# Memory columns between columns of z, weights in pieces of four blocks, six split pairs and a queue model with GpSimd's hold

## The chip, the core and the metric

The kernel runs on one core of a Trainium2 chip. The metric is the device time of one execution in microseconds (us). Engines: PE is TensorE (PEld its weight loads), DVE is VectorE, ACT is ScalarE, POOL is GpSimd, SP is SyncE, on whose queue all transfers are issued here. A block is 128 rows or columns.

## What is computed

One layer of a decoder, for a prompt of 512 tokens and a sample of 8 tokens, which lie side by side as 520 columns. Float32 throughout.

```python
h = rms_norm(x, norm_g);  z = h @ w_in          # 2048 -> 56 blocks of 128 columns
u, gate_pool, qkv (3 groups x q,k,v x 4 heads), gate_dil, q_mem (4 heads), gate_mem = split(z)
mem_kv = rms_norm(mem_prompt, mem_norm_g) @ w_mem_kv        # 256 memory tokens, 8 blocks
y_pool = pool_mix(u)                                        # trailing means 2, 4, 8, 16
y_dil  = 3 groups of banded attention (window, dilation) = (128,1), (512,4), (2048,16), QK-norm, merged per head
y_mem  = attention of q_mem on the memory tokens, QK-norm
y = x + concat(silu(gate_pool)*y_pool, silu(gate_dil)*y_dil, silu(gate_mem)*y_mem) @ w_out   # 12 blocks -> 16 blocks
```

The sample does the same with its own caches, which are copied to the outputs shifted by one row. Outputs are y, the new keys and values, the memory's keys and values and the shifted caches.

## The kernel before

**Layout.** Channels are on the partitions, tokens in the free dimension. A job makes one block of 128 columns of z (or of the memory's keys and values, or of the output): it goes through the 16 blocks of the inner dimension (12 for the output). Each float32 product is done as three products in fp32r: weights and activations are split in a high and a low part, and high times high, high times low and low times high are added. A job of z has 2 sections of 260 columns, so 16 x 3 x 2 = 96 matmuls; a job of the memory has one section of 256 columns and 48 matmuls; a job of the output has 72. There are 56 jobs of z, 8 of the memory and 16 of the output.

**The weights' way.** `emit_raw` loads raw weights into a ring `wraw`. `emit_split` takes four blocks (512 columns) of them: ACT writes the high part `whi`, DVE the low part `wlo` (raw less high). I call this a split; there are 304. One split serves 24 matmuls of a job of z (a piece), or 12 of the memory. The pairs `whi`, `wlo` lie in a ring of `SPB` = 5. `run_jobs` emits one split after each piece, so a split stands in the program three pieces ahead of its use. `wraw` has `RAWB` = 6 tiles of eight blocks (512 KB). When a tile's second half has been split, the next load is issued on SP, and with it, at a rate, copies of the caches (`d2d_q`, up to 712 KB each).

**What sets the order.** The program is in manual order: each engine runs its instructions in the order in which the Python code emits them. Side work (norms, attention, the sample) is written as generators in `tasks`. After each block `tick` advances those whose last step is done by the clock `ck`, a model of the five queues: `use` adds a duration to an engine's queue, and `busy` holds tasks back when ACT or DVE has over 2.5 us of queue beyond PE. `p_ar` is GpSimd's sum or maximum over the partitions, in place, 96 of them; the model books it on `pool` alone.

**Stages.** `run_first` does four jobs of z at once, while the squares of x are summed; then come four jobs (q and k of head 0), during which `mem_prep` scales and splits the memory; then the 8 jobs of the memory, back to back; then 8 gates, and for each head its v, q and k, with `mem_attn`, `dil_attn` and the sample's units (`sample_scores`, `sample_values`; 16 for the memory, 16 for the heads) between them; then the pool's jobs; then the output. The output's first two jobs run together, block by block, since the blocks of y come ready late. An evacuation of a finished job (`q_evac`, `mem_evac`, ...) waits in `pend`, in order of jobs. A dot product of the sample is `sk` (product on DVE), `p_ar(sk)`, `smx` (maximum, DVE), exponentials (ACT), then eleven small DVE instructions (`sz`, `ss`, `sy`, `sv`).

Of the kernel before, what the change touches and what calls it, by code (L numbers as in the profile page):

```python
# [26 lines left out]
NH = 4  # L27
# [21 lines left out]
class Clock:  # L49


    LAT = 0.12

    def __init__(self):
        self.pe = 0.0
        self.free = {"act": 0.0, "dve": 0.0, "pool": 0.0, "sp": 0.0, "hbm": 0.0}
        self.last = 0.0
        self.written = {}
        self.used = {}

# [18 lines left out]
    def use(self, eng, dur, ins, outs):  # L79
# [13 lines left out]
        end = max(self.free[eng], self.after(ins, outs)) + dur  # L93
        self.free[eng] = end
        self.done(end + self.LAT, ins, outs)

# [18 lines left out]
def trunk(ctx, tc, nc, I, O):  # L115
# [66 lines left out]
    def d_red(out, in_, op, axis):  # L182
        nc.vector.tensor_reduce(out=out, in_=in_, op=op, axis=axis)  # L183
        ck.use("dve", nfree(in_) * 0.00104 + 0.08, [in_], [out])
# [7 lines left out]
    def d_recip(out, in_):  # L192
        nc.vector.reciprocal(out=out, in_=in_)
        ck.use("dve", nfree(out) * 0.0083 + 0.08, [in_], [out])
# [59 lines left out]
    free = {"tmp": 3, "sq": 2, "vt": 2, "psb": 4}  # L254
# [76 lines left out]
    def job(src, nkb, lhs, sections, done, wide=True):  # L331
        jobs.append((src, nkb, lhs, sections, done, wide))

    raws = []
    quarters = []
# [4 lines left out]
    RAWB = 6  # L340
    SPREAD = 8
    SPB = 5
# [4 lines left out]
    def build_stream():  # L347

        def pair(j0):
            for k in range(0, jobs[j0][1], 4):  # L350
                for j in (j0, j0 + 1):
                    raws.append((jobs[j][0][:, k:k + 4, :], 4))
                    quarters.append(((j, k), 0, len(raws) - 1))

        for k0, k1 in [(0, 1), (1, 2)] + [(k, k + 2) for k in range(2, KB, 2)]:
            raws.append((I["w_first"][:, FIRST * k0:FIRST * k1, :], FIRST * (k1 - k0)))
            for k in range(k0, k1):
                quarters.append((("first", k), FIRST * (k - k0), len(raws) - 1))
        for j in range(FIRST, len(jobs)):
            nkb = jobs[j][1]  # L360
            if j == first_o:
                pair(j)
            if j in (first_o, first_o + 1):
                continue
            for k0 in range(0, nkb, 8):
                n = min(8, nkb - k0)
                raws.append((jobs[j][0][:, k0:k0 + n, :], n))
                for q in range(k0, k0 + n, 4):
                    quarters.append(((j, q), q - k0, len(raws) - 1))

    def emit_raw():
# [3 lines left out]
        src, n = raws[i]  # L375
# [11 lines left out]
    def emit_split():  # L387
        i = nxt_q[0]
        if i >= len(quarters):
            return  # L390
        nxt_q[0] += 1
        key, off, ri = quarters[i]
        r = raw_t[ri][:, off:off + 4, :]
# [4 lines left out]
        split_t[key] = (hi, lo)  # L398
        if i + 1 >= len(quarters) or quarters[i + 1][2] != ri:
            del raw_t[ri]  # L400
            emit_raw()
# [7 lines left out]
    def run_jobs(group, each=None, before=None):  # L409
        accs = {}  # L410
        for j in group:
            _, _, _, sections, _, wide = jobs[j]
            if wide:
                t = psum_m()
                accs[j] = [t[:, s, 0:c1 - c0] for s, (c0, c1) in enumerate(sections)]
            else:
# [4 lines left out]
        nkb = jobs[group[0]][1]  # L421
        cur = {}
        for k in range(nkb):
            if before:
                before(k)
            for j in group:
                _, _, lhs, sections, _, _ = jobs[j]
                if k % 4 == 0:
                    cur[j] = split_t.pop((j, k))
                whi, wlo = cur[j]  # L430
                mh, ml = lhs(k)
                for a, b, w, m in ((0, 0, whi, mh), (0, 1, whi, ml), (1, 0, wlo, mh)):
                    for s, (c0, c1) in enumerate(sections):
                        mm(accs[j][s], w[:, k % 4, :], m[:, c0:c1],
                           start=(k == 0 and a == 0 and b == 0), stop=(k == nkb - 1 and a == 1))
            if each:
                each(k)
            if k % 4 == 3:
                for _ in group:
                    emit_split()  # L440
            if flags.get("x"):
                while pend and (flags.get("mem") or pend[0][0]):
                    pend.pop(0)[1]()
            tick()
        for j in group:
            pend.append((len(jobs[j][3]) == 2, lambda j=j: jobs[j][4](accs[j])))
# [71 lines left out]
    def mem_evac(i):  # L518
# [12 lines left out]
        def value(acc):  # L531
            need("vt")
            z = row("vt", 2)[:, 0:ML]
# [90 lines left out]
    def v_evac(g, h):  # L624
        def f(acc):
            need("vt")
            z = row("vt", 2)
# [290 lines left out]
    def pool_task(c, u):  # L918
# [5 lines left out]
        while sh < w:  # L924
            nt_ = row("vt", 2)
# [70 lines left out]
    def zjob(cb, done, wide=True):  # L996
        job(I["w_in"][cb], KB, xs, SEC, done, wide)

    for h in range(NH):
        zjob(CB_QM + h, q_first(h), h < 2)  # L1000

    def qk_jobs(h, groups):
        for g in groups:
            zjob(CB_QKV + g * 12 + h, q_evac(g, h))
            zjob(CB_QKV + g * 12 + 4 + h, k_evac(g, h))

    qk_jobs(0, (0, 1))
    first_m = len(jobs)
    for i in range(NM):
        job(I["w_mem"][i], KB, lambda k: (memt[k // 2][0][:, k % 2, :], memt[k // 2][1][:, k % 2, :]),  # L1010
            ((0, ML),), mem_evac(i), False)
    first_q = len(jobs)
    for h in range(NH):
        zjob(CB_GM + h, gate_evac(8 + h, 4 if h == 3 else 0))
    for h in range(NH):
        zjob(CB_GD + h, gate_evac(4 + h, 4 if h == 3 else 0))
    for h in range(NH):
        for g in range(NG):
            zjob(CB_QKV + g * 12 + 8 + h, v_evac(g, h))
        qk_jobs(h, range(NG) if h else (2,))  # L1020
    for c in range(4):
        zjob(CB_GP + c, gate_evac(c, 4 if c == 3 else 0))
    for c in (3, 2, 1, 0):
        zjob(CB_U + c, u_evac(c))
    first_o = len(jobs)
    for m in range(NO):
        job(I["w_out"][m], KO, xs, SEC, o_evac(m), m != 1)
# [13 lines left out]
    RATE = len(d2d_q) / (2.0 * (first_o - first_q) + 1.5 * SPREAD)  # L1041


    with tc.manual_schedule():
# [11 lines left out]
        load_x(1)  # L1056
        emit_raw()
        load_x(2)
        emit_raw()
        load_x(3)  # L1060
        load_x(4)
        emit_raw()
        load_x(5)
        load_x(6)
        emit_raw()
        load_x(7)
# [123 lines left out]
        run_first(each_first)  # L1190
        while not flags.get("x"):
            push()
        j = FIRST
        while j < len(jobs):
            if j == FIRST:
                spawn(mem_prep())
                mem_task = tasks[-1]
            if j == FIRST + 1:
# [5 lines left out]
            if j == first_m:  # L1204
# [3 lines left out]
            if j == first_q:  # L1208
# [3 lines left out]
            if j == first_o - 1:  # L1212
                run_jobs([j], lambda k: split_ready(k))
            elif j == first_o:
# [112 lines left out]
```

## Time and profile before

| | us |
|---|---|
| time before, median of 3 runs | 927.62 (927.02 to 927.92) |
| the profiled execution, its own time | 927.79 |
| its span in the trace | 926.0 |
| PE busy | 894.7 (97%) |
| DVE busy | 672.9 (73%) |
| ACT busy | 388.2 (42%) |
| POOL busy | 285.0 (31%) |
| the 16 DMA engines, mean share | 68.4% |

The span lies 1.8 us under the execution's own time. Ends of matmuls are modelled and overlap, so PE's 97% is not the share of the time in which it could not have been faster; the distance from one start to the next is what a matmul takes. A duration on DVE includes the time for which the instruction was held up after its start.

### The profile page before, as it was taken

How to read it: one execution, taken by the hardware profiler on the slowest of the kernel's cores; microseconds unless marked ns; L12 is line 12 of the kernel's file. 1: busy time of each engine (PE TensorE's matmuls, PEld its weight loads, DVE VectorE, ACT ScalarE, POOL GpSimd, SP SyncE). 2: the span in 40 equal slices, each digit the busy share in tenths (PEclk: the TensorE clock that was granted, in tenths of full speed). 3: DMA queues.
4: the chain of work that ended last, by engine and by line, in shares of the span. 5: the costliest groups of instructions: out<-in, count | busy, mean ns of one | idle time of the engine just before them, and what ended most of it. 6: DMA issues, size and time to landing. Idle time of an engine off the chain costs nothing.

```text
span 926.0 us, 17968 instructions
## 1 busy us (share of the span) xinstructions
PE 894.7 (97%) x7208; PEld 879.2 (95%) x7208; DVE 672.9 (73%) x1225; ACT 388.2 (42%) x795; POOL 285.0 (31%) x96
## 2 busy tenths in 40 slices
PE   7999898999999999999999999989999999999998
PEld 7999888999999999999998999989999899999998
DVE  7678999757888769977698866997659698333231
ACT  7547655443364434444343353245432624222220
POOL 1032544325444424622255322552215220000000
PEclk9999999999999999999999999999999999999999
DMA  9435346897877866578866788668975545899531
GB/s 347 157 114 196 115 154 224 270 341 233 275 222 258 289 223 212 195 260 311 289 233 217 271 300 311 218 221 285 332 253 195 211 137 197 329 389 352 196 104 47
DMA packets 64211, 219.52 MB, mean 237 GB/s; under 512 B 8440, under 2 KB 22648, under 8 KB 61944
## 3 DMA queue, kind: packets, MB, share of 16 engines
q1 hardware_dynamic: 64128, 218.39, 68.4%
q8 instruction: 56, 0.92, 0.4%
q14 instruction: 27, 0.22, 0.1%
HBM read 200.32 MB, written 106.25 MB: 331 GB/s over the span
## 4 chain that ended last, share of the span: by engine, by line
PE 70%; DVE 22%; ACT 3%; issue 3%; DMA 2%; POOL 0%; SPq 0%; DVEq 0%; ACTq 0%
PE psm L205 62%; PE psb L205 8%; DVE wlo L164 7%; DVE sv L187 3%; DVE mx L164 2%; DVE S L164 2%; DVE smx L183 1%; DVE sk L164 1%; ACT whi L154 1%; ACT sk L154 1%; DVE tmp L168 1%; DMA o_kv<-vt 1%; DVE vt L164 1%; DVE qk L164 1%; DVE smx L168 1%
## 5 line engine op out<-in xcount | busy, mean ns | idle before, releaser
L205 PE MATMUL psm<-xh,whi 128*128 128x260 f32 x2088 | 434.0, 288 | 9.2 <-ACT whi L154 8.4
L205 PE MATMUL psm<-xh,wlo 128*128 128x260 f32 x2088 | 426.2, 285 | 9.7 <-DVE wlo L164 9.7
L205 PE MATMUL psm<-xl,whi 128*128 128x260 f32 x2088 | 423.9, 284 | 0.0
L205 PEld LDWEIGHTS psm<-xh,whi 128*128 128x128 f32 x2088 | 326.2, 190 | 16.1 <-ACT whi L154 8.6
L164 DVE TENSOR_TENSOR wlo<-wraw,whi 128x512 fp32r<-128x512 f32 x304 | 270.4, 906 | 96.5 <-ACT whi L154 96.1
L205 PEld LDWEIGHTS psm<-xh,wlo 128*128 128x128 f32 x2088 | 324.8, 190 | 12.1 <-DVE wlo L164 12.0
L205 PEld LDWEIGHTS psm<-xl,whi 128*128 128x128 f32 x2088 | 324.4, 190 | 0.0
L154 ACT ACTIVATE whi<-wraw 128x512 fp32r<-128x512 f32 x304 | 181.0, 621 | 169.0 <-PE psm L205 149.3
L197 POOL PARTITION_ALL_REDUCE sk<-sk x32 | 130.3, 4071 | 130.3 <-DVE sk L164 56.1
L197 POOL PARTITION_ALL_REDUCE sq<-sq x32 | 101.0, 3164 | 186.2 <-ACT sq L154 186.2
L154 ACT ACTIVATE sk<-sk,smx 128x256 f32<-128x256 f32 (+1 forms) x64 | 35.5, 555 | 115.3 <-DVE smx L168 64.8
L197 POOL PARTITION_ALL_REDUCE mx<-mx x17 | 46.4, 2729 | 69.7 <-DVE mx L164 69.3
L164 DVE TENSOR_TENSOR tmp<-psm,vn 128x260 f32<-128x260 f32 x30 | 11.5, 424 | 76.8 <-PE psm L205 58.5
L154 ACT ACTIVATE tmp<-tmp 128x520 f32<-128x520 f32 (+2 forms) x76 | 46.3, 610 | 23.8 <-DVE sq L168 16.5
L154 ACT ACTIVATE sq<-qk 128x520 f32<-128x520 f32 x28 | 17.7, 636 | 85.9 <-DVE qk L164 77.9
L205 PE MATMUL psb<-y,wlo 128*128 128x256 f32 x128 | 37.7, 295 | 6.9 <-DVE wlo L164 6.9
L205 PE MATMUL psb<-y,whi 128*128 128x256 f32 x192 | 42.6, 290 | 0.8 <-ACT whi L154 0.8
L154 ACT ACTIVATE tmp<-sq,eps 128x520 f32<-128x520 f32 (+1 forms) x32 | 22.3, 696 | 33.2 <-POOL sq L197 33.2
L205 PEld LDWEIGHTS psb<-y,whi 128*128 128x128 f32 x192 | 32.9, 196 | 1.0 <-ACT whi L154 1.0
L187 DVE CUSTOM_DVE_ANT_1 sv<-sv,sk,sy 128x384 f32<-128x384 f32 x32 | 33.1, 1071 | 0.6
L205 PEld LDWEIGHTS psb<-y,wlo 128*128 128x128 f32 x128 | 24.9, 194 | 8.9 <-DVE wlo L164 8.8
L168 DVE SCALAR_TENSOR_TENSOR tmp<-sq,tmp 128x520 f32<-128x520 f32 (+1 forms) x32 | 21.6, 675 | 11.6 <-ACT tmp L154 11.6
(129 smaller groups left out, 740.8 us busy)
## 6 DMA issues: line engine op xcount, KB each, us to landing
o_cache<-cache SPq DMA_DIRECT2D x88, 712.0 KB, 7.9
wraw<-w_in SPq DMA_DIRECT2D x104, 512.0 KB, 5.3
o_cache<-cache SPq DMA_DIRECT2D x24, 584.0 KB, 6.6
vn<-xT SPq DMA_DIRECT2D x32, 260.0 KB, 5.7
wraw<-w_mem SPq DMA_DIRECT2D x16, 512.0 KB, 4.0
wraw<-w_out SPq DMA_DIRECT2D x14, 512.0 KB, 6.5
o_zero<-zero SPq DMA_DIRECT2D x6, 1024.0 KB, 8.8
sk<-dks SPq DMA_DIRECT2D x16, 384.0 KB, 3.0
```

Source lines behind the costliest of these rows:

```text
L154: nc.scalar.activation(out=out, in_=in_, func=func, scale=scale, bias=bias, **kw)
L164: nc.vector.tensor_tensor(out=out, in0=in0, in1=in1, op=op)
L168: nc.vector.scalar_tensor_tensor(out=out, in0=in0, scalar=scalar, in1=in1, op0=op0, op1=op1)
L183: nc.vector.tensor_reduce(out=out, in_=in_, op=op, axis=axis)
L187: nc.vector.tensor_tensor_reduce(out=out, in0=in0, in1=in1, scale=1.0, scalar=init, op0=op0, op1=op1, accum_out=accum)
L197: nc.gpsimd.partition_all_reduce(t, t, P, op)
L205: nc.tensor.matmul(out, lhsT=lhsT, rhs=rhs, start=start, stop=stop)
```

## The change

Five things are changed together.

1. **Order of jobs.** Jobs are grouped by hand as lists of pieces (`groups`). The memory's 8 jobs no longer run back to back: each of four jobs of z (v of group 0 and 1, k of group 1, v of group 2, all head 0) is cut in its four pieces, and between these stand the pieces of two memory jobs. So three jobs of z precede the memory instead of four, and three jobs of v move from after it to between it. `mem_prep` is put first among the tasks and starts one group after the first.
2. **Pieces of weights.** `wraw` holds four blocks (256 KB) instead of eight, in 10 tiles instead of 6; each split frees its tile and issues the next load. Loads of weights go from 163 to 304 and all DMA issues from 472 to 613. The copies' rate is set anew.
3. **Six pairs** (`SPB` 5 to 6), and three tiles `vt` instead of two.
4. **The model.** `p_ar` calls `hold`: for the inner part of its duration the model's DVE does not start an instruction, except for those that read PSUM and for reductions and reciprocals. A matmul of 260 columns is 0.120 us in the model instead of 0.111, `p_ar` 10% shorter.
5. **Evacuations.** `pend` lets an evacuation of z pass one of the memory that still waits for the memory's norm. The output's first two jobs alternate by pieces of four blocks instead of by blocks.

```diff
-        ck.use("pool", nfree(t) * 0.00625 + 0.35, [t], [t])
+        ck.use("pool", nfree(t) * 0.00563 + 0.35, [t], [t])
+        e = ck.free["pool"]
+        ck.hold(e - nfree(t) * 0.00563 - 0.1, e - 1.15)
...
+    def hold(self, s, e):
+
+        if s < self.free["dve"]:
+            self.free["dve"] += e - s
+        self.held = [h for h in self.held if h[1] > self.pe] + [(s, e)]
...
-        d = 2 * max(0.107, n / 1200.0) if lhsT.dtype == F32 else max(0.107, (n + 6) / 2400.0)
+        d = 2 * max(0.107, n / 1200.0) if lhsT.dtype == F32 else max(0.107, n * 0.000456 + 0.0015)
...
-    RAWB = 6
+    RAWB = 10
     SPREAD = 8
-    SPB = 5
+    SPB = 6
...
-        t = st([P, 8, P], "wraw", RAWB)
-        load(t[:, 0:n, :], src)
-        raw_t[i] = t
-        d2d["acc"] += d2d["rate"] * n / 8.0
+        raw_t[i] = st([P, 4, P], "wraw", RAWB)
+        load(raw_t[i], raws[i][1])
+        d2d["acc"] += d2d["rate"]
...
-                while pend and (flags.get("mem") or pend[0][0]):
-                    pend.pop(0)[1]()
+                    for p in [p for p in pend if p[0] or flags.get("mem")]:
+                        pend.remove(p)
+                        p[1]()
...
+    for i, (f, a) in enumerate(((v_job, (0, 0)), (v_job, (1, 0)), (k_job, (1, 0)), (v_job, (2, 0)))):
+        j = f(*a)
+        m0, m1 = mem_job(2 * i), mem_job(2 * i + 1)
+        groups.append([(j, 0), (m0, 0), (m0, 4), (j, 4), (m0, 8), (m0, 12),
+                       (j, 8), (m1, 0), (m1, 4), (j, 12), (m1, 8), (m1, 12)])
...
-    RATE = len(d2d_q) / (2.0 * (first_o - first_q) + 1.5 * SPREAD)
+    RATE = len(d2d_q) / (4.0 * (last_g - first_q) + 3.0 * SPREAD)
...
-                spawn(mem_prep())
-                mem_task = tasks[-1]
+                mem_task = [ck.pe, mem_prep()]
+                tasks.insert(0, mem_task)
```

**SP's queue in the memory's stage.** A row is a transfer, out<-in and shape; `w_mem` are the memory's weights, `w_in` those of z. Before:

```order
L215 DMA wraw_1031<-w_mem 128x1024
L215 DMA wraw_1096<-w_mem 128x1024
L215 DMA vn_1154<-memT 128x512
L215 DMA wraw_1172<-w_mem 128x1024
L215 DMA vn_1238<-memT 128x512
L215 DMA wraw_1250<-w_mem 128x1024
```

The same queue in the changed kernel:

```order
L230 DMA sv_973<-mvs 128x512
L230 DMA wraw_1007<-w_mem 128x512
L230 DMA wraw_1054<-w_in 128x512
L230 DMA wraw_1092<-w_mem 128x512
L230 DMA wraw_1131<-w_mem 128x512
L230 DMA wraw_1165<-w_in 128x512
```

The tiles are half as large, a piece of z stands before each two of the memory, and the memory's own columns (`memT`) have moved ahead of this place.

**DVE's queue at head 2.** Here `sk` is the product whose partition sum POOL takes next, `sz` to `y` are one unit of the sample, `wlo` is a split. Before, from the product to the next split:

```order
L164 TENSOR_TENSOR sk_7439<-sk_7439,qs_82 128x768
L164 TENSOR_TENSOR sz_7516<-sz_7516,szs_7517 128x2
L193 RECIPROCAL sz_7516<-sz_7516 128x2
L164 TENSOR_TENSOR ss_7056<-ss_7056,cs_84 128x3x2
L183 TENSOR_REDUCE sy_1080_7519<-ss_7056 128x2
L187 ISA sv_7287,sy_7518<-sv_7287,sk_7285,sy_1080_7519 128x3x128
L187 ISA sy_7518 128x1
L187 ISA sv_7287,sy_7518<-sv_7287,sk_7285,sy_1080_7519 128x3x128
L187 ISA sy_7518 128x1
L164 TENSOR_TENSOR sy_7518<-sy_7518,sz_7516 128x2
L164 TENSOR_TENSOR y_513_3144<-y_513_3144,sy_7518 128x2
L164 TENSOR_TENSOR wlo_7598<-wraw_7052,whi_7597 128x512
```

The changed kernel, around the corresponding product:

```order
L177 TENSOR_TENSOR wlo_7812<-wraw_7405,whi_7811 128x512
L196 TENSOR_REDUCE smx_7830<-sk_7570 128x2
L181 SCALAR_TENSOR_TENSOR smx_7830<-smx_7830,nself_7242 128x2
L177 TENSOR_TENSOR wlo_7856<-wraw_7442,whi_7855 128x512
L177 TENSOR_TENSOR sk_7732<-sk_7732,qs_82 128x768
L177 TENSOR_TENSOR wlo_7888<-wraw_7473,whi_7887 128x512
L177 TENSOR_TENSOR qk_7901<-psm_7749,rsx_72 128x260 x2
L177 TENSOR_TENSOR wlo_7935<-wraw_7513,whi_7934 128x512
```

Before, the unit's small instructions and the evacuation of a job stood between the product and the split, so that the split came last of all; now splits stand directly behind the maximum and behind the product, and the unit has moved to another gap.

**PE's queue at the output's first two jobs.** `psm` and `psb` are the sums of the two jobs, `xh` and `xl` the split blocks of y. Before:

```order
L205 MATMUL psm_9517<-xh_24_87,whi_9441 128x260 x2
L205 MATMUL psm_9517<-xl_40_103,whi_9441 128x260 x2
L205 MATMUL psm_9517<-xh_24_87,wlo_9442 128x260 x2
L205 MATMUL psb_9518<-xh_24_87,whi_9479 128x260
L205 MATMUL psb_9519<-xh_24_87,whi_9479 128x260
L205 MATMUL psb_9518<-xl_40_103,whi_9479 128x260
```

The changed kernel:

```order
L220 MATMUL psm_9780<-xh_24_87,whi_9692 128x260 x2
L220 MATMUL psm_9780<-xl_40_103,whi_9692 128x260 x2
L220 MATMUL psm_9780<-xh_24_87,wlo_9693 128x260 x2
L220 MATMUL psm_9780<-xh_25_88,whi_9692 128x260 x2
L220 MATMUL psm_9780<-xl_41_104,whi_9692 128x260 x2
L220 MATMUL psm_9780<-xh_25_88,wlo_9693 128x260 x2
```

Before, the second job used block 0 of y before block 1 was touched; now the first job goes through blocks 0 to 3 before the second begins.

## Rows read from the trace of the kernel before

**Rows 1.** Chain of work that ended last, merged: start us, us, what.

```profile
6.24 2.98 PE psm L205 x12
...
54.33 46.13 PE psm L205 x384
100.46 2.84 PE psb L205 x24
...
158.48 1.43 PE psm L205 x12
...
454.15 0.89 PE psb L205 x8
...
458.81 0.86 PE psb L205 x4
...
918.41 4.57 PE psm L205 x36
```

**Rows 2.** Timeline of PE, first score matmuls of heads 0 to 3.

```profile
337.97 1.05 PE L205 MATMUL psb<-qk,qk 128*128 128x128 f32 x8
...
453.99 1.05 PE L205 MATMUL psb<-qk,qk 128*128 128x128 f32 x8
...
571.96 1.05 PE L205 MATMUL psb<-qk,qk 128*128 128x128 f32 x8
...
689.17 1.05 PE L205 MATMUL psb<-qk,qk 128*128 128x128 f32 x8
```

**Rows 3.** Stretches: us, busy PE, PEld, DVE, ACT, POOL, PEclk, DMA share, GB/s.

```profile
54.00:100.00 46.00, 46.00 (x385) 46.00 (x385) 42.55 (x68) 29.53 (x57) 13.44 (x4) 1.00 0.51 167
100.00:158.00 58.00, 50.23 (x390) 48.10 (x390) 55.22 (x87) 33.64 (x69) 30.29 (x11) 0.97 0.49 162
...
478.00:532.00 54.00, 50.41 (x398) 49.35 (x397) 47.52 (x85) 22.58 (x52) 22.74 (x6) 0.97 0.74 254
```

**Rows 4.** Waits: engine, line, waited for: us in total, times, longest.

```profile
ACT whi L154 <- PE psm L205: 149.3, 70, 4.4
...
ACT sk L154 <- DVE smx L168: 64.8, 12, 10.1
...
PE psm L205 <- DVE wlo L164: 9.7, 9, 2.6
```

**Rows 5.** Timeline at head 2, rows of POOL, DVE and PE.

```profile
617.05 4.67 POOL L197 PARTITION_ALL_REDUCE sk<-sk  x1 [8.73 <-DVE sz L164]
...
617.36 3.49 DVE L187 CUSTOM_DVE_ANT_1 sv<-sv,sk,sy 128x384 f32<-128x384 f32 x1
...
620.78 0.61 DVE L187 CUSTOM_DVE_ANT_1 sv<-sv,sk,sy 128x384 f32<-128x384 f32 x1
...
624.58 0.80 PE L205 MATMUL psm<-xh,wlo 128*128 128x260 f32 x2 [2.59 <-DVE wlo L164]
```

**Rows 6.** One row of DVE's timeline, a split's low part without a hold.

```profile
612.88 0.68 DVE L164 TENSOR_TENSOR wlo<-wraw,whi 128x512 fp32r<-128x512 f32 x1
```

**Rows 7.** Timeline at head 3, one row of ACT and one of PE.

```profile
731.54 0.62 ACT L154 ACTIVATE sk<-sk,smx 128x384 f32<-128x384 f32 x1 [7.52 <-DVE smx L168]
...
738.93 0.51 PE L205 MATMUL psm<-xh,whi 128*128 128x260 f32 x2 [2.18 <-ACT whi L154]
```

**Rows 8.** DMA: two issues (count, KB, us to landing), two stretches as in rows 3.

```profile
wraw<-w_out SPq DMA_DIRECT2D x14, 512.0 KB, 6.5
...
wraw<-w_out SPq DMA_DIRECT2D x20, 256.0 KB, 6.9
...
6.00:12.00 6.00, 5.76 (x33) 5.76 (x34) 5.62 (x10) 5.68 (x11) 0.52 (x4) 1.00 1.03 396
...
816.00:830.00 14.00, 14.00 (x118) 14.00 (x118) 4.62 (x9) 2.89 (x5) 0.00 (x0) 1.00 1.03 421
```

**Rows 9.** Timeline at the last block of y, two rows of DVE.

```profile
789.30 0.93 DVE L168 SCALAR_TENSOR_TENSOR y<-psb,gains,y 128x260 f32<-128x260 f32 x2 [0.80 <-PE psb L205]
...
790.94 0.70 DVE L164 TENSOR_TENSOR xl<-y,xh 128x520 fp32r<-128x520 f32 x1 [0.70 <-ACT xh L154]
```

More of the change, by code (lines that the diff above doesn't have):

```diff
@@ L59, in __init__ @@
         self.used = {}
+        self.held = []
     def after(self, ins, outs):
@@ L92, in use @@
             return
-        end = max(self.free[eng], self.after(ins, outs)) + dur
+        start = max(self.free[eng], self.after(ins, outs))
+        if eng == "dve" and shared and not any(a.tensor.name.startswith("ps") for a in ins):
+            for s, e in self.held:
+                if s <= start < e:
+                    start = e
+        end = start + dur
         self.free[eng] = end
         self.done(end + self.LAT, ins, outs)
+    def hold(self, s, e):
+        if s < self.free["dve"]:
+            self.free["dve"] += e - s
+        self.held = [h for h in self.held if h[1] > self.pe] + [(s, e)]
     def dma(self, nbytes, ins, outs):
@@ L347, in build_stream @@
     def build_stream():
[L349 to L369, printed above, removed]
+        for k in range(KB):
+            raws.append((("first", k), I["w_first"][:, FIRST * k:FIRST * k + FIRST, :]))
+        for seq in groups[1:]:
+            for j, k in seq:
+                raws.append(((j, k), jobs[j][0][:, k:k + 4, :]))
     def emit_raw():
@@ L407, in flush_pend, with run_jobs @@
             pend.pop(0)[1]()
[L409 to L413, printed above, removed]
+    accs = {}
+    def run_jobs(seq, each=None, before=None):
+        fin = [] if before else pend
+        for j, q in seq:
+            _, nkb, lhs, sections, done, wide = jobs[j]
+            if q == 0 and wide:
                 t = psum_m()
                 accs[j] = [t[:, s, 0:c1 - c0] for s, (c0, c1) in enumerate(sections)]
-            else:
+            elif q == 0:
                 need("psb", len(sections))
@@ L1012, in trunk, with group, mem_job, q_job @@
-    first_q = len(jobs)
+        return job(I["w_in"][cb], KB, xs, SEC, done, wide)
+    def group(*js):
+        groups.append([(j, q) for q in range(0, jobs[js[0]][1], 4) for j in js])
+    def mem_job(i):
+        return job(I["w_mem"][i], KB, lambda k: (memt[k // 2][0][:, k % 2, :], memt[k // 2][1][:, k % 2, :]),
+                   ((0, ML),), mem_evac(i), False)
+    def q_job(g, h):
+        return zjob(CB_QKV + g * 12 + h, q_evac(g, h))
+    def k_job(g, h):
+        return zjob(CB_QKV + g * 12 + 4 + h, k_evac(g, h))
@@ L1055, in trunk @@
         load(gains, I["gains"])
-        load_x(1)
+        for k in range(1, 8):
+            load_x(k)
+            emit_raw()
         emit_raw()
[L1058 to L1066, printed above, removed]
         emit_raw()
@@ L1188, in need_split @@
                     push()
[L1190 to L1195, printed above, removed]
-                spawn(mem_prep())
-                mem_task = tasks[-1]
-            if j == FIRST + 1:
+        for gi, seq in enumerate(groups):
+            if gi == 1:
+                mem_task = [ck.pe, mem_prep()]
+                tasks.insert(0, mem_task)
+            if gi == 2:
                 consts()
```

132 lines of the change are left out of this document (65 added, 67 removed).

## The prediction

> **What bounds the kernel now.** I read the chain of waits first. It is PE nearly from end to end: matmuls of 260 columns that follow each other every 46.13 / 384 = 0.1201 us, of 256 columns every 2.84 / 24 = 0.1183 us, and in attention 0.111 us (128 columns) and 0.215 us (256) [rows 1]. So the question is not which engine is busiest but how much of PE's time is not work. With these four steps I priced PE's whole queue: 878 us from the first matmul at 6.24 to the end of the last, 918.41 + 4.57 = 922.98. That is 916.7 us, so some 38 us are lost. The table of stretches and the start of each head's first score matmul say where.
>
> - Start: 1.6 us.
> - Memory: its stage runs from 100.46 to 158.48 [rows 1], 58.0 us, for 384 x 0.1183 = 45.4 us of matmuls and 0.6 of others: 12.0 lost.
> - Heads: the four marks lie 116.0, 118.0 and 117.2 us apart [rows 2]. A head is nine jobs of z (864 x 0.1201 = 103.8), 36 x 0.111 = 4.0, 12 x 0.215 = 2.6 and transposes of 1.2, together 111.6: lost 4.4 to 6.4 each (4.6 for the first, whose transposes differ). From the last mark to 922.98 are 233.8 us for 226.3 of work: 7.5 lost, of which about 5.1 before and 2.4 in the output. Another 0.4 goes before the first mark.
>
> So 12.0 + 0.4 + 4.6 + 6.4 + 5.6 + 5.1 = **34.1 us** are lost in places that the change rearranges; the start and the output's 2.4 stay.
>
> Then I asked what PE waits for. In the memory's stage DVE is busy 55.22 of 58 us, where the four jobs of z before it left it at 42.55 of 46, and PE's clock has fallen to 0.97 of its upper level of 2.4 GHz [rows 3]. In the heads DVE has idle time (47.52 of 54 busy), yet PE still waits: the list of waits puts 9.7 us on `wlo` [rows 4]. The rows at head 2 show the way: GpSimd's sum of 768 columns starts at 617.05; DVE's `sv`, begun at 617.36, takes 3.49 us where the same instruction behind it takes 0.61, so the sum holds DVE for 2.88 us; the unit's small instructions follow, and PE goes on 2.59 us late [rows 5]. At head 3 the same chain runs through ACT: an exponential waits 7.52 us for DVE's `smx`, the split behind it on ACT comes late, and PE waits 2.18 us [rows 7]. Such a stop costs more than itself, since the clock stands at 0.97 in the stretch around it [rows 3].
>
> **The change part by part.**
>
> *Order of the memory's pieces.* A job of z needs four splits in 11.5 us of PE, one of the memory four in 5.7. I walked DVE's queue with a split at 0.64 us (mean of those not held; [rows 6] has one of 0.68), each sum's hold as it fell in the trace, the rest at their rows. Before, splits 35 to 63: 29 x 0.64 = 18.6, 26.7 of others, 13.8 for nine holds, 59.1 us, against 47.7 of PE: 11.4 short, and the trace lost 12.0. So the walk is good to about 0.6. In the new order the worst stretch is splits 41 to 73: 33 x 0.64 = 21.1, 32.3 of others, 13 holds at 1.4 = 18.2, together 71.6 against 71.6 of PE. The loss goes to about nothing, but with no room. From below it is 0. From above, DVE idled 2.8 of the 58 us in which it was the bound [rows 3], 5%; 5% of 71.6 is 3.5, with the walk's 0.6 about 4. I take **1.5**, nearer to 0, since the sixth pair can carry work over the worst place.
>
> *Six pairs.* ACT waits 149.3 us in 70 waits for PE to release a pair [rows 4]: it is the number of pairs that stops splits from running ahead. One more is one more piece, 24 x 0.1201 = 2.88 us, as long as the hold of [rows 5]. By the walk five pairs would leave the new memory's stage 1.6 us short and head 0 0.6.
>
> *The model and the new places.* In the model a sum now delays DVE, so side work on DVE is put later and splits come first. The order shows it at head 2: splits directly behind `smx` and behind `sk`. By the walk the heads were 3.4, 2.7 and 5.5 us short before (heads 0 to 2); now all have slack, 2.3 us at head 0, 7.2 and 7.3 at heads 1 and 2, 5.6 at head 3. What stays is ACT's queue, which no walk of DVE covers: `sk` on ACT waited 64.8 us for `smx` in 12 waits [rows 4], and a split may still stand behind one. From below 0; from above one stop of [rows 7] a head, 2.18 each, 8.7. I take 0.75 a head, **3.0**, nearer to 0, since six pairs give 2.88 us more before such a stop reaches PE.
>
> *Half-size loads.* 141 more transfers on SP. SP is on no path: a load's tile is now freed by each split, and the lead of 10 pieces is 28.8 us (it was 11, 31.7; some 19 among the memory's short pieces), while a load of 256 KB lands 6.9 us after its issue and one of 512 KB after 6.5 [rows 8]. The two rows say that landing does not follow size, and that half of a load is cheap only while transfers overlap. They do: with loads of 260 to 512 KB from 6 to 12 us the engines moved 396 GB/s, against 421 in the output's stretch [rows 8]. I take 0; what it costs if that cover fails is a rival below.
>
> The Trainium skill speaks against this edit: "DMA: Bandwidth & Descriptors", section "Bandwidth", wants transfers of 1 MiB or more, and its anatomy section fits about 2.0 us fixed to each. If that were paid one after the other, 141 more would be 282 us of DMA time. By that rule the heads would be bound by transfers and the time lie beyond rival C's below; here [rows 8] disagrees, with 396 GB/s at a quarter to half of that size.
>
> *`mem_prep` first, `memT` earlier, third `vt`, evacuations.* The memory's columns are issued one split earlier and land in time as before; a `vt` more only removes a wait. The passing evacuation frees a sum bank that would otherwise wait for the memory's norm. 0 each.
>
> *The output's pair by four blocks.* Block 11 of y is needed 19 x 6 x 0.1201 = 13.7 us after the pair starts, before 22 x 6 x 0.1201 = 15.9. In the new order 20 matmuls, 2.4 us, lie between the last pool matmul and the first use of the last low part; the chain from DVE's `y` at 789.30 to the end of `xl` at 791.64 takes 2.34 [rows 9]. That just fits; one wait as in those rows (0.70) would show. From 0 to 1; I take **0.5**.
>
> **The sum.** Span 926.0 - 34.1 + 1.5 + 3.0 + 0.5 = 896.9; with the 1.8 between span and own time 898.7; the profiled execution lies 0.17 above the median, so **898.5 us**. With none of the three 893.5; with all at their upper ends (4, 8.7, 1) 907. The forecast's own range is 893 to 906.
>
> **The rivals.**
>
> *A. The heads keep their stops.* If ACT's order (exponential behind `smx` behind a sum) and not DVE's decides, two thirds of the heads' 21.7 stay: 14.5 instead of 3, about 911; with a memory's stage at its upper end 915. For it: 64.8 us of ACT's waits [rows 4] and DVE's 12% of idle time at head 2 [rows 3]. Against: before, the splits behind the unit were the last thing PE waited for [rows 5]. 906 to 920.
>
> *B. The memory's stage stays bound by DVE.* The walk ends at 0 with no room, and the twelve jobs run together over 4 x 11.53 + 46.0 = 92 us. If DVE idles 5% there (4.6), and holds are 1.6 and not 1.4 (2.6, as in [rows 5] in proportion to columns 1.95), 7 to 8 us stay: about 905, 902 to 910. For it: 55.22 of 58 [rows 3]. Against: the walk gave 11.4 for 12.0.
>
> *C. Slower: the small loads become the bound.* At head 2 the transfers are 0.74 busy and move 254 GB/s [rows 3]; taken for all 595 us from the memory's end to the pool's last jobs, that is 440 us of DMA work. Weights are 1 MB per 11.53 us, 91 GB/s, 36% of it, 158 us. If a load of half the size took as long as a whole one, that doubles: 598 us, and at a share of 0.97 616, against 573 of PE after the gain. The splits then wait for loads (ACT's `whi` on a transfer, which is not there now), 43 us more: about 937. It decides once a half costs some 80% more per byte. [rows 8] shows 6% (396 against 421), so this needs what no row shows, SP's queue standing behind the 712 KB copies.
>
> *D. No change.* The new order moves the stops elsewhere, and the model's hold is wrong as often as right: 920 to 929. Against: sixth pair and memory's order do not rest on the model.
>
> **How the numbers follow.** Forecast 0.66, A 0.15, B 0.10, C 0.05, D 0.04. A measurement of this kernel tells about 0.2%, 1.9 us, from no change. Faster by more than that: 0.66 + 0.15 + 0.10 and 0.01 of D, 0.92; within it 0.03; slower 0.05. 892 to 912 holds the forecast with 1 us below its zero, B, and nearly half of A: about 0.8.
>
> **What would show it.** Right: 12 jobs from the first piece of memory to the last in 92 to 94 us; marks of the heads 111.6 to 112.5 apart; PE's clock 1.00 in every stretch after the start; `wlo` and `whi` gone from PE's waits; ACT's waits on PE for a pair well over 149 us. A: marks still 115 apart, `sk` on `smx` near 65. B: DVE over 95% busy and `wlo` before PE only among the memory. C: `whi` waiting for transfers, landings over 10 us, share near 1. Wrong altogether: DVE's holds not where sums are, so that slack in the walk means nothing.

## The result and the profile after

The changed kernel takes **897.24 us** (median of 4, 896.30 to 897.78), against 927.70 of before on the same chip (927.02 to 927.92): a ratio of 0.967, 95% interval 0.9655 to 0.9689, 30 us less. The forecast was 898.5 (892 to 912). The profiled execution has a span of 894.6 us, where before it had 926.0.

The waits of the kernel after (engine, line, waited for: us in total, times, longest):

```profile
ACT whi L167 <- PE psm L220: 142.3, 65, 4.0
...
ACT sk L167 <- DVE smx L187: 37.0, 9, 8.7
ACT sk L167 <- DVE smx L181: 32.5, 9, 8.6
...
PE psm L220 <- DVE wlo L177: 2.3, 3, 1.2
```

PE's 9.7 us on `wlo` [rows 4] have become 2.3, in three stops. The memory's own matmuls (`psb`) had waited 6.9 us more, and that line is gone:

```profile
PE psb L205 <- DVE wlo L164: 6.9, 8, 1.8
```

ACT's `sk` waits 32.5 us on the form of `smx` of [rows 4], where it was 64.8, and 37.0 on the other, where it was 45.2. ACT waits for a pair no longer than before (142.3 against 149.3), though splits that ran ahead through all six pairs would wait longer for a free one: a first sign against the pairs.

The stretches (us, busy PE, PEld, DVE, ACT, POOL, PEclk, DMA share, GB/s): three jobs of z before the memory, the memory's stage with its four jobs of z, and a stretch of the heads that answers to the second heads' stretch in [rows 3]:

```profile
54.00:88.00 34.00, 34.00 (x286) 34.00 (x285) 31.20 (x49) 23.81 (x47) 12.95 (x4) 1.00 0.46 161
88.00:184.00 96.00, 93.65 (x784) 93.03 (x783) 87.66 (x152) 54.20 (x114) 45.07 (x15) 1.00 0.52 164
465.00:519.00 54.00, 53.95 (x446) 53.58 (x446) 46.48 (x84) 23.51 (x53) 22.64 (x6) 1.00 0.83 283
```

In the memory's stage PE is busy 93.65 of 96 us, where it had 50.23 of 58, and the clock is at its upper level in all three stretches. In the heads DVE is about as busy as before (46.48 against 47.52 us) and PE loses 0.05 us instead of 3.6. DVE has the same 1225 instructions as before; they stand elsewhere in its queue, and over the whole span it is busy 647.3 us instead of 672.9, since less of its work falls under a sum. Head 2 shows how (start us, us, what; left out behind `y` are the unit's short instructions):

```profile
585.22 0.68 DVE L177 TENSOR_TENSOR wlo<-wraw,whi 128x512 fp32r<-128x512 f32 x1
585.82 0.95 DVE L177 TENSOR_TENSOR sk<-sk,qs 128x768 f32<-128x768 f32 x1
586.92 4.67 POOL L210 PARTITION_ALL_REDUCE sk<-sk  x1 [0.65 <-DVE sk L177]
589.11 0.69 DVE L177 TENSOR_TENSOR y<-y,psb 128x512 f32<-128x512 f32 x1 [2.34 <-PE psb L220]
...
592.30 0.69 DVE L177 TENSOR_TENSOR wlo<-wraw,whi 128x512 fp32r<-128x512 f32 x1
```

The sum of 768 columns takes 4.67 us as in [rows 5], but a split stands in front of the product. Nearly half of the sum passes while DVE waits 2.34 us for PE anyway, and `y`, which reads PE's result, runs under it in 0.69 us. The next split comes at 592.30, and PE does not wait for it.

What is left lies among the memory. The chain of waits before the last of the three stops (start us, us, what):

```profile
172.42 2.06 DVE tmp L181
...
174.96 0.50 DVE kmem L181
...
175.48 0.03 ACT sq L167
...
176.02 0.62 ACT whi L167
...
176.67 2.37 DVE wlo L177
179.05 0.04 issue
179.09 1.00 PE psm L220 x6
```

The sum under the last of these rows of DVE:

```profile
176.21 3.28 POOL L210 PARTITION_ALL_REDUCE sq<-sq  x1 [1.03 <-ACT sq L167]
```

The chain goes through two queues. On ACT the split's high part `whi` stands behind `sq`, which waits for DVE's `kmem`; then the low part, 0.68 us in [rows 6], takes 2.37, held by the sum, and PE goes on behind it. Loads of 256 KB land sooner than in [rows 8] (count, KB each, us to landing), and no split waits for one:

```profile
wraw<-w_in SPq DMA_DIRECT2D x208, 256.0 KB, 5.4
...
wraw<-w_out SPq DMA_DIRECT2D x48, 256.0 KB, 5.0
```

### The profile page after: what moved, and what is told of

Its sections match the earlier page's. It is cut to its first block, busy times and chain, and to the rows that moved or that the text cites. A ratio compares the mean times of both kernels' runs of the same rounds, so it can differ in the third digit from the quotient of the medians.

```text
span 894.6 us, 18350 instructions
## 1 busy us (share of the span) xinstructions
PE 882.3 (99%) x7208; PEld 871.6 (97%) x7208; DVE 647.3 (72%) x1225; ACT 388.7 (43%) x795; POOL 286.6 (32%) x96
## 4 chain that ended last, share of the span: by engine, by line
PE 94%; DVE 4%; issue 1%; DMA 0%; ACT 0%; SPq 0%; DVEq 0%; ACTq 0%
PE psm L220 81%; PE psb L220 12%; DVE wlo L177 1%; DVE sv L200 1%; PE psb L226 1%; DVE tmp L181 1%; DVE sq L181 0%; DVE sk L177 0%; DMA gains<-gains 0%; DVE vt L177 0%; DVE qk L177 0%; DVE smx L196 0%; ACT whi L167 0%; DVE tmp L177 0%; SPq L230 0%
## 5 line engine op out<-in xcount | busy, mean ns | idle before, releaser
L177 DVE TENSOR_TENSOR wlo<-wraw,whi 128x512 fp32r<-128x512 f32 x304 | 248.7, 838 | 50.5 <-ACT whi L167 50.4
L167 ACT ACTIVATE whi<-wraw 128x512 fp32r<-128x512 f32 x304 | 180.2, 622 | 172.4 <-PE psm L220 142.3
L210 POOL PARTITION_ALL_REDUCE sq<-sq x32 | 102.8, 3215 | 128.3 <-ACT sq L167 128.3
L177 DVE TENSOR_TENSOR qk<-psm,rsx 128x260 f32<-128x260 f32 x56 | 21.3, 421 | 22.7 <-PE psm L220 22.7
L220 PE MATMUL psb<-y,wlo 128*128 128x256 f32 x128 | 35.9, 281 | 0.0
L200 DVE CUSTOM_DVE_ANT_1 sv<-sv,sk,sy 128x384 f32<-128x384 f32 x32 | 31.1, 1009 | 0.6
L181 DVE SCALAR_TENSOR_TENSOR qk<-qk,gains_r,sq 128x520 f32<-128x520 f32 x28 | 27.7, 988 | 1.0
```

The source lines that it names most:

```text
L167: nc.scalar.activation(out=out, in_=in_, func=func, scale=scale, bias=bias, **kw)
L177: nc.vector.tensor_tensor(out=out, in0=in0, in1=in1, op=op)
L181: nc.vector.scalar_tensor_tensor(out=out, in0=in0, scalar=scalar, in1=in1, op0=op0, op1=op1)
L200: nc.vector.tensor_tensor_reduce(out=out, in0=in0, in1=in1, scale=1.0, scalar=init, op0=op0, op1=op1, accum_out=accum)
```

## The experiments

Each run stands as its ratio to the kernel before on the same chip, and as us against before worked out from that (ratio less 1, times 926.8).

| run | median us | ratio (95%) | us against before |
|---|---|---|---|
| the changed kernel | 897.24 | 0.9672 (0.9655 to 0.9689) | -30.4 |
| five_pairs | 896.57 | 0.9673 (0.9658 to 0.9687) | -30.3 |
| old_model | 916.22 | 0.9889 (0.9874 to 0.9904) | -10.3 |
| memory_in_a_row | 902.66 | 0.9738 (0.9722 to 0.9754) | -24.3 |
| before_small_loads | 924.15 | 0.9976 (0.9966 to 0.9986) | -2.2 |
| before_new_model | 904.85 | 0.9761 (0.9742 to 0.9780) | -22.2 |
| no_hold | 936.27 | 1.0103 (1.0084 to 1.0123) | +9.5 |
| five_pairs_old_model | 919.93 | 0.9927 (0.9909 to 0.9945) | -6.8 |
| before_small_loads_six | 922.42 | 0.9951 (0.9935 to 0.9967) | -4.5 |
| extra_sums_memory | 904.27 | 0.9755 (0.9739 to 0.9772) | -22.7 |
| extra_sums_heads | 900.86 | 0.9722 (0.9708 to 0.9735) | -25.8 |
| before_hold_alone | 937.87 | 1.0118 (1.0104 to 1.0132) | +10.9 |
| memory_over_five | 894.23 | 0.9649 (0.9635 to 0.9662) | -32.5 |

**One part of the change taken back.** First the pairs.

```diff
-    SPB = 6
+    SPB = 5
```

> The changed kernel with five pairs instead of six. Theory (a walk of DVE's queue against PE's, with a split at 0.64 us and the holds of GpSimd's sums, as in the prediction): the memory's stage is 3.0 us short and head 0 1.7, the others keep 2.8 us of slack or more, so 4 to 6 us over the changed kernel's 897.2: 901 to 903. Rival (pairs): the sixth pair is what removed the heads' stops, the new order did little there; then the four heads fall back by some 2.9 us each and the memory by 3, about 911.

896.57: the same as with six. Theory and rival both missed. PE's waits on `wlo` are no longer than with six:

```profile
ACT whi L167 <- PE psm L220: 192.1, 94, 4.1
...
PE psm L220 <- DVE wlo L177: 1.6, 2, 0.9
```

ACT waits for pairs longer (192.1 us), and it costs nothing. The 3.0 and 1.7 us by which the walk found it short (memory and head 0), against about 0 and a slack of 2.3 with six, did not come out. DVE is busy 670.6 us with the same 1225 instructions, 23 more than with six pairs, and no time is lost by it: what counts is where a hold falls. The program sees the ring's size in its clock and places side work anew, so DVE's order differs between the two runs.

Then the model (in five_pairs_old_model with `SPB = 5` besides).

```diff
-        ck.use("pool", nfree(t) * 0.00563 + 0.35, [t], [t])
-        e = ck.free["pool"]
-        ck.hold(e - nfree(t) * 0.00563 - 0.1, e - 1.15)
+        ck.use("pool", nfree(t) * 0.00625 + 0.35, [t], [t])
...
-        d = 2 * max(0.107, n / 1200.0) if lhsT.dtype == F32 else max(0.107, n * 0.000456 + 0.0015)
+        d = 2 * max(0.107, n / 1200.0) if lhsT.dtype == F32 else max(0.107, (n + 6) / 2400.0)
```

> The changed kernel with the old model: no hold on DVE, a matmul at 0.111 us, GpSimd's sums at their old price; jobs, pieces and six pairs stay. Theory: the walk finds the memory's stage 5.3 us short, head 0 1.7, the gates 0.6, heads 1 to 3 just not short: 7 to 10 us over 897.2, 904 to 908, most of it among the memory. Rival (pairs): the model's places matter little once six pairs are there, within 2 us of 897.2. Rival (model alone): the model is the whole gain of the heads, 15 to 20 us back, about 915.

916.22: 20 us come back, the total of the rival (model alone), and twice what the walk gave. But not all of it is in the heads, as that rival had it. By PE's start times some 8 of the 20 us are lost among the memory, though its pieces still stand between those of z. The stretch of the memory's stage:

```profile
88.00:192.00 104.00, 96.94 (x786) 95.24 (x785) 95.99 (x167) 56.64 (x123) 49.48 (x17) 0.98 0.50 159
```

PE is idle 7.06 us in it, where the changed kernel has 2.35. In the heads the stops are back too, and look as in [rows 5]; here are a sum on POOL and DVE at head 1, and PE's row behind them:

```profile
501.28 0.15 DVE L177 TENSOR_TENSOR sz<-sz,szs 128x2 f32<-128x2 f32 x1
...
502.00 3.68 POOL L210 PARTITION_ALL_REDUCE sq<-sq  x1
502.47 2.63 DVE L200 CUSTOM_DVE_ANT_1 sv<-sv,sk,sy 128x384 f32<-128x384 f32 x1
...
505.41 1.29 DVE L177 TENSOR_TENSOR wlo<-wraw,whi 128x512 fp32r<-128x512 f32 x2
506.16 0.51 PE L218 MATMUL psm<-xh,wlo 128*128 128x260 f32 x2 [1.63 <-DVE wlo L177]
```

The unit from `sz` on, with `sv` held (2.63 us; 0.61 without a hold in [rows 5]), again stands before the splits.

> The changed kernel with five pairs and the old model: of the change only the order of the memory, the loads of four blocks, the third vt and the evacuations stay. Theory (pairs matter where the model puts side work ahead of splits): the walk finds 6.1 us short among the memory and 6.6, 5.2, 2.7 and 0.6 in the heads, 13 us more than with six pairs and the old model (916.2): 924 to 930, no faster than before. Rival (a sixth pair is worth nothing, as five against six with the new model, 896.6 against 897.2): 915 to 918.

919.93, between the two: with the old model the sixth pair is worth 3.5 us, a quarter of the walk's 13. By PE's start times that is a net: with six pairs some 7 us less are lost behind the memory and 3 more in it. Here too the program places side work anew for each size of the ring, so this is not the pair alone.

The memory's order, with the jobs of v behind the gates again:

```diff
+    group(k_job(1, 0))
     first_m = len(groups)
-    for i, (f, a) in enumerate(((v_job, (0, 0)), (v_job, (1, 0)), (k_job, (1, 0)), (v_job, (2, 0)))):
...
+    for i in range(NM):
+        group(mem_job(i))
...
```

> The changed kernel with the memory's eight jobs back to back after four jobs of z, and the jobs of v behind the gates, as before; model, pieces and pairs stay. Theory: the walk finds the memory's stage 5.5 us short and every head with slack: 5 to 7 us over 897.2, 902 to 904; the heads' marks as in the changed kernel. Rival (order of the memory decides it): the 12 us of the kernel before come back less the 2.9 of one more pair, 9 us, about 906. Rival (the model alone would have mended the stage): within 2 us of 897.2.

902.66, as the theory said: 6 us come back, in PE's stops among the memory:

```profile
PE psb L220 <- DVE wlo L177: 5.1, 4, 3.5
```

With the new model the interleaving itself is worth half of the 12.0 of the stage. The other half is taken up below, where the model is changed alone.

**One part of the change alone.**

```diff
-    RAWB = 6
+    RAWB = 10
...
-        t = st([P, 8, P], "wraw", RAWB)
+        t = st([P, 4, P], "wraw", RAWB)
...
-            for k0 in range(0, nkb, 8):
-                n = min(8, nkb - k0)
+            for k0 in range(0, nkb, 4):
+                n = min(4, nkb - k0)
...
```

Not shown: the weights of the first four jobs come in loads of four blocks too, in turn with the loads of x.

> The kernel before with weights in pieces of four blocks in 10 tiles, each freed by its own split (304 loads of weights instead of 163), and nothing else. Theory: small loads cost nothing and gain nothing, the walk finds the same stops (11.4 among the memory; 2.9, 5.2, 5.2 and 0.6 in the heads, before 3.4, 2.7, 5.5 and 1.1): 925 to 931. Rival (transfers): a small load costs as much as a large one, splits wait for loads, 950 or more. Rival (small loads free tiles earlier and are a part of the gain): 920 or less.

924.15, 2.2 us less than before, just under what was expected. Small loads cost nothing; why they gain a little was not settled (stops moved between heads, and PE's stop on ACT's `whi` at head 3 [rows 7] is gone).

> The kernel before with loads of four blocks in 10 tiles and six pairs; old model, old order of jobs. Theory: the walk finds every stage 2.9 us less short than with five (8.4 among the memory; 0.0, 2.3, 2.3, none in the heads; sum 13 instead of 25), so 10 to 12 us less than the 924.2 of the same with five pairs: 912 to 915. Rival (a sixth pair is worth nothing): 922 to 926.

922.42, another 2.3 us and not 10 to 12. The trace says why. PE's two longest stops take 3.16 us each with five pairs and 3.15 with six. The second of them, with five:

```profile
625.30 0.80 PE L205 MATMUL psm<-xh,wlo 128*128 128x260 f32 x2 [3.16 <-DVE wlo L164]
```

And with six:

```profile
624.07 0.51 PE L205 MATMUL psm<-xh,wlo 128*128 128x260 f32 x2 [3.15 <-DVE wlo L164]
```

The same to 0.01 us. Ahead of it DVE ran some 47 us without a gap of over 0.5 us, and what it last waited for was this (five pairs, then six):

```profile
578.53 0.76 DVE L164 TENSOR_TENSOR S<-psb,masks 128x256 f32<-128x256 f32 x2 [0.73 <-PE psb L205]
```

```profile
577.31 0.76 DVE L164 TENSOR_TENSOR S<-psb,masks 128x256 f32<-128x256 f32 x2 [0.73 <-PE psb L205]
```

It is the head's scores, a result of PE, that DVE waits for, not a free pair. From there to the stop DVE runs the same 81 instructions in the same order in both runs, 11 of them splits. `SPB` only sizes the ring; `emit_split` stands once behind each piece either way. DVE's queue is in order, so splits can't run ahead past what stands before them, however many pairs are free.

The model alone, in the old order and with five pairs (the diff of the model above, put into the kernel before, with the class `Clock` of the changed one and its exceptions for reductions and reciprocals):

> The kernel before with the new model alone (GpSimd's hold on DVE, a matmul at 0.120 us, GpSimd's sums 10% shorter); order of jobs, loads of eight blocks and five pairs stay. Theory, as it stands after the run with the old model (916.2, 19 over the changed kernel): the model is what removes the heads' stops, with five pairs as well. The walk finds 9.6 us short among the memory and every head with slack of 2.5 us or more, so the 22 us of the heads go and 10 to 12 stay: 904 to 909. Rival (the parts need each other): without the sixth pair or the memory's new order the model brings half of that, 915 or more.

904.85, as the theory said: **the model alone is worth 22 us.** The two stretches that answer to the second and third of [rows 3]:

```profile
100.00:158.00 58.00, 50.26 (x403) 49.14 (x402) 54.92 (x87) 34.82 (x70) 28.26 (x10) 0.97 0.52 171
465.00:519.00 54.00, 54.00 (x449) 53.84 (x448) 43.82 (x94) 24.84 (x56) 23.21 (x7) 1.00 0.83 296
```

The heads lose nothing; the memory's stage loses what it lost before (50.26 busy, was 50.23). So the model alone mends the heads. The memory needs both it and the interleaving. PE's waits in the memory's stage (us, the sum of its lines of the list of waits), all with six pairs and small loads:

| | old model | new model |
|---|---|---|
| memory back to back | 7.8 (before_small_loads_six) | 5.1 (memory_in_a_row) |
| memory between z | 7.0 (old_model) | 2.3 (the changed kernel) |

With the old model the interleaving takes away less than 1 us of stops. The first of these runs also lacks `mem_prep` put first, the third `vt` and the passing evacuations, which no run tells apart.

**The model's two parts.** The hold taken out of the changed kernel, the new prices kept:

```diff
-        e = ck.free["pool"]
-        ck.hold(e - nfree(t) * 0.00563 - 0.1, e - 1.15)
```

> The changed kernel with GpSimd's hold taken out of the model; the new prices of a matmul and of GpSimd's sums stay. Theory: the hold is what the model's gain rests on. Without it, and with PE's price right, the model sees less of a queue on DVE and puts side work earlier still: the walk finds 10.3 us short among the memory, 0.8, 0.7, 2.3 and 0.4 in the heads, more than with the whole old model (5.3, 1.7, -0.3, -0.2), which ran at 916.2: 915 to 925. Rival (the price of a matmul is what mended the model): 897 to 903.

936.27, slower than before and beyond the theory's range. PE now waits for side work as well as for splits:

```profile
PE psb L224 <- DVE vt L177: 11.2, 6, 4.0
...
PE psm L218 <- DVE wlo L177: 9.3, 8, 3.2
...
PE psb L218 <- ACT S L167: 4.3, 3, 3.1
```

And the other way, the hold put into the kernel before with the old prices:

> The kernel before with GpSimd's hold in the model, and the old prices of a matmul and of GpSimd's sums. Theory (hold and price must go together: the hold puts side work later, and a PE that is too fast in the model lets DVE look late, so that side work comes later still): every head has slack (1.2 us or more), 8.7 us are short among the memory, but side work piles up behind the heads, where the walk finds 28 us short at the output's beginning: 905 and up to 28 more, 915 to 935, with PE's stops at the pool's last jobs and the output's first. Rival (the hold alone is the gain): 903 to 907, as with the whole new model.

937.87, just over the theory's range, and in the place that it named. PE's rows at the output's beginning, and the stretch:

```profile
777.21 2.10 PE L220 MATMUL psb<-vt,kmem 128*128 128x260 f32 x4 [13.27 <-DVE y L181]
782.22 2.10 PE L220 MATMUL psb<-vt,kmem 128*128 128x260 f32 x4 [2.91 <-DVE y L181]
...
800.28 0.80 PE L220 MATMUL psm<-xh,whi 128*128 128x260 f32 x2 [11.05 <-ACT xh L167]
```

```profile
745.00:800.00 55.00, 27.12 (x177) 24.28 (x176) 47.55 (x106) 14.38 (x43) 18.19 (x4) 0.76 0.41 152
```

27 us of stops, and PE's granted clock is 0.76 in the stretch. The heads run without a stop, but their side work is put off until nothing is left to hide it behind. Hold and price are one correction, as the two expectations argued: with the hold alone the model sees DVE too late, with the price alone too early. (The price alone was tried only in the new order, the hold alone only in the old one; the prices of a matmul and of a sum were not tried apart.)

**The hold by itself.** Sums on a tile that no one reads, with the other engines' order unchanged:

```diff
                 if k % 4 == 3:
                     emit_split()
+                    if (j, q) in extra:
+                        nc.gpsimd.partition_all_reduce(spare, spare, P, RADD)
...
```

> The changed kernel with four more sums on GpSimd, of 448 columns of a spare tile that nobody reads, one in each group of the memory's stage; the model does not see them, and the order of DVE, ACT and PE is word for word that of the changed kernel. Theory (a sum holds DVE, and DVE has no room among the memory): in proportion to columns a hold is 448 / 768 x 2.88 = 1.7 us, 6.7 for four, of which most comes out at PE, with the later sums behind them: 3 to 7 us over the changed kernel, 900 to 904. Rival (a hold matters only where somebody waits for that very sum): within 1 us of 897.

> The same with 14 more such sums, one in every second job of the heads and none among the memory. Theory (heads have slack): 14 x 1.7 = 24 us of holds, some 6 in a head against 13 to 14 us of DVE's idle time there, so 0 to 3 us over the changed kernel, 897 to 900, less than four sums cost among the memory. Rival (each hold comes out at PE wherever it falls): 915 or more.

Four sums among the memory: 904.27, 7.7 us more against before, just beyond the theory's 3 to 7. Fourteen in the heads: 900.86, 4.6 more, over its 0 to 3 but less than four cost among the memory, and far from 915. Busy times on the pages of the changed kernel, of four sums more and of 14 more:

```profile
PE 882.3 (99%) x7208; PEld 871.6 (97%) x7208; DVE 647.3 (72%) x1225; ACT 388.7 (43%) x795; POOL 286.6 (32%) x96
```

```profile
PE 886.1 (98%) x7208; PEld 874.2 (97%) x7208; DVE 654.2 (72%) x1225; ACT 388.1 (43%) x795; POOL 300.3 (33%) x101
```

```profile
PE 884.8 (98%) x7208; PEld 873.8 (97%) x7208; DVE 670.4 (75%) x1225; ACT 388.0 (43%) x795; POOL 331.7 (37%) x111
```

DVE runs the same 1225 instructions in the same order, and is busy 6.9 us longer for four sums and 23.1 for 14, 1.7 us for each: the hold in proportion to columns. Among the memory all of it comes out at PE. In the heads 23 us of holds make one stop of note, in head 0, to which the prediction's walk had given the least slack (2.3 us); one of 0.35 us at 508.21 is the only other:

```profile
376.22 0.80 PE L220 MATMUL psm<-xh,wlo 128*128 128x260 f32 x2 [2.03 <-DVE wlo L177]
```

```profile
345.00:400.00 55.00, 52.97 (x416) 51.65 (x415) 51.66 (x85) 24.59 (x59) 30.12 (x8) 0.97 0.65 221
```

The clock is 0.97 in that stretch, as around the stops of [rows 3]. From 376 to 381 alone it is 0.66 (a mean over the levels of 1.2 and 2.4 GHz), and from 376.82 to 379.42 PE's pairs of matmuls start 0.43 us apart instead of 0.24. By PE's start times this stop costs near 4 us with what follows.

**The memory spread further.** The memory's 32 pieces spread evenly over five jobs of z.

```diff
-    group(q_job(1, 0))
     first_m = len(groups)
-    for i, (f, a) in enumerate(((v_job, (0, 0)), (v_job, (1, 0)), (k_job, (1, 0)), (v_job, (2, 0)))):
...
+    zs = [f(*a) for f, a in ((q_job, (1, 0)), (v_job, (0, 0)), (v_job, (1, 0)), (k_job, (1, 0)), (v_job, (2, 0)))]
+    ms = [(j, k) for j in [mem_job(i) for i in range(NM)] for k in range(0, KB, 4)]
+    for i, j in enumerate(zs):
+        seq = []
+        for k in range(0, KB, 4):
+            seq.append((j, k))
+            n = i * 4 + k // 4 + 1
+            while len(ms) > 32 - (32 * n) // 20:
+                seq.append(ms.pop(0))
+        groups.append(seq)
```

> The changed kernel with the memory's 32 pieces spread over five jobs of z instead of four (q of group 1 joins them), evenly. Theory (what is left of the changed kernel's loss lies among the memory, stops of 0.32, 1.35 and 1.16 us, and the walk gives 0.6 us more room): 894 to 896.5. Rival (mem_prep, which now has one job less to itself, comes late or the walk's 0.6 means nothing): 897 to 899.

894.23, 2.1 us less against before than the changed kernel. Its memory's stage and its only wait of PE of note, the one at the start:

```profile
88.00:184.00 96.00, 96.00 (x809) 96.00 (x808) 87.46 (x156) 55.75 (x117) 45.45 (x16) 1.00 0.53 169
```

```profile
PE psm L220 <- ACT whi L167: 6.5, 1, 6.5
```

PE has no stop among the memory any more; DVE is as busy as in the changed kernel (87.46 against 87.66 us). The two intervals of the ratios overlap by a little, so the times alone do not settle the 2.1 us; that the 2.3 us of stops are gone stands in the traces.

## Why the prediction was right, and where not

**The total.** The forecast span was 896.9, measured 894.6. Of the 34.1 us lost, most is gone, as forecast. By the terms (loss is read from how far PE's start times run behind its priced work; where a stage ends, to some tenths of a us):

| term | forecast us | measured us |
|---|---|---|
| left among the memory | 1.5 (0 to 4) | 3.1 |
| left in the heads | 3.0 (0 to 8.7) | 1.9 |
| last block of y | 0.5 (0 to 1) | 0 |
| output, taken as unchanged | 2.4 | 1.3 |

The rest of the 2.3 us, about 1, is in the start and in the pricing of PE's queue. That the total came out so near is in part luck: the memory kept 1.6 us more than forecast, the other terms 2.7 less.

**The memory.** Right in that DVE was the bound and that the new order takes the bound away "with no room"; four extra sums showed that there was none. Two things were wrong. The value was too low because the sixth pair was to "carry work over the worst place", and it does not. And rival D's "sixth pair and memory's order do not rest on the model" is false for the order: with the old model the interleaved stage keeps 7.0 us of stops against 2.3. Of the signs, `wlo` did not go from PE's waits (three stops are left, all in this stage, where rival B looked for them; but 3.1 us and not its 7 to 8). The twelve jobs, counted from the piece of z that stands first, take 96 us instead of the 92 to 94 forecast (93.2 from the first piece of the memory itself).

**The heads.** Right: splits ahead of the unit, and PE's waits on `wlo` vanish. Before_new_model shows that the model alone does it, and with the heads' stops rival A falls. ACT's waits on `smx`, on which A rested, say little either way: memory_over_five has 50.3 us on the form of [rows 4] and no stop. The reading of [rows 5] was short by a row. Behind the hold of `sv` came a second sum, which held the split itself:

```profile
621.63 3.36 POOL L197 PARTITION_ALL_REDUCE sq<-sq  x1
621.71 4.03 DVE L164 TENSOR_TENSOR wlo<-wraw,whi 128x512 fp32r<-128x512 f32 x3
```

The three splits take 4.03 us; at 0.68 to the first and 0.6 for each behind it (1.29 for two at 505.41 in old_model) they would take 1.9. So PE's stop there comes from two holds, 2.88 and some 2.1 us, and not from one. The sign of the marks was no sign: the first score matmuls lie 64.2, 109.1 and 110.9 us apart now, since they stand elsewhere in PE's queue. The clock is 1.00 in every stretch, as forecast.

**Six pairs: wrong.** The sentence "it is the number of pairs that stops splits from running ahead" was read from ACT's 149.3 us of waits [rows 4]. These are waits of an engine that is early. At the stop shown for before_small_loads, DVE had been running without a break since a result of PE, in the same order with five pairs as with six. Five pairs with the new model give the same time, and six in the old order 2.3 us. The forecast that these waits would go "well over 149 us" failed too (142.3). That the total was near in spite of it is because the new model had in the walk already all the slack that the heads needed. The prediction's "1.6 us short" with five pairs does not follow from its own numbers either: 71.6 against 71.6 less 2.88 for a pair is 2.9.

**The walk.** Its size was right to about 3 us a stage at best: about 0 for 3.1 lost, five pairs 3.0 for some 2.5, before_new_model 9.6 for about 10.6. Its order among the kernels was right only in part: it put no_hold (915 to 925) under five_pairs_old_model (924 to 930), and they took 936.27 and 919.93. Where DVE was just not short (old_model, heads 1 and 2), PE stopped for 1.6 us each. Slack of less than 3 us in it means nothing.

**Half-size loads.** Right: cover holds, and rival C falls (share 0.83 in the heads and no split waiting for a load; from 184 to 250 us the share is 0.96, with PE busy 66.00 of 66). 141 transfers more in before_small_loads left the time 2.2 us lower. The Trainium skill ("DMA: Bandwidth & Descriptors", section "Bandwidth") asks for batches of 1 MiB or more, measured there on transfers that GpSimd issues. Here SP issues them, they overlap, and neither a price for halving them nor the prediction's 282 us shows in any row.

**The last block of y** just fitted, as worked out. Its low part is done at 764.70 + 0.70 = 765.40, and PE takes it 0.30 us later, without a wait:

```profile
764.70 0.70 DVE L177 TENSOR_TENSOR xl<-y,xh 128x520 fp32r<-128x520 f32 x1 [0.70 <-ACT xh L167]
...
765.70 0.41 PE L220 MATMUL psm<-xl,whi 128*128 128x260 f32 x2
```

**A sum of rival A** is off: 898.5 with 14.5 instead of 3.0 in the heads is 910, not 911, and 912.5 with the memory at its upper end, not 915. The forecast does not rest on it.

## What to carry to other kernels

A planner is only as good as its price of what engines do to each other: a few lines for GpSimd's hold on DVE, together with a truer price for PE, were worth more here (22 us) than a new order, more buffers and smaller loads taken together (10), and either half alone made the kernel slower. The new order paid only once the model was right. Long waits of an early engine for a buffer don't say that more buffers help; ask what the engine that is late last waited for. Where a short stage needs one engine at twice the rate of its neighbours, interleave it widely: over four jobs 2.3 us of stops were left here, over five none.

## What was not expected of the hardware

A sum over the partitions holds DVE although no one reads or writes the same data: 1.7 us for 448 columns on a spare tile (23.1 us for 14 sums), as 2.9 for 768 [rows 5]. The row of one sum on POOL, and DVE's two splits under it, which take 3.04 us where such a pair took 1.29 (at 505.41 in old_model):

```profile
547.87 3.05 POOL L433 PARTITION_ALL_REDUCE spare<-spare  x1
```

```profile
547.50 3.04 DVE L177 TENSOR_TENSOR wlo<-wraw,whi 128x512 fp32r<-128x512 f32 x2
```
